# Attention's opening by halves of its heads, a fixed matmul order in two closings, and a row scale that shares a PSUM bank

## The chip, the cores and the metric

The kernel runs on one core of a Trainium2 chip. The metric is the device time of one execution in microseconds, the median of three runs. The engines are TensorE (PE in the profile, with PEld for its weight loads), VectorE (DVE), ScalarE (ACT), GpSimd (POOL) and SyncE (SP, whose queue SPq issues most DMAs). Each engine works through its own instruction list in order and waits where an operand is not ready.

## The reference, cut to what matters

One inference step of a two-layer trunk, for one prompt of 1024 tokens (16 learned meta tokens ahead) and eight samples of 4 new tokens with a paged cache.

```python
x = x + conv_module(x);  x = x + conv_ffn(rms_norm(x))         # layer 0
hn = rms_norm(h, kv_norm)
c  = rms_norm(hn @ w_dkv, lat_norm)                            # shared latent, 128 wide
kr = rope(rms_norm(hn @ w_kr, knorm_rope), pos)                # shared rotary key, 32 wide
q  = rms_norm(xn @ w_dq, q_lat_norm) @ w_uq                    # 16 heads of 64 + 32
q_nope = rms_norm(q[..., :64]);  q_rope = rope(rms_norm(q[..., 64:]), pos)
k_nope = rms_norm(c @ w_uk);  v = c @ w_uv
o  = softmax((q_nope @ k_nope + q_rope @ kr) * SM_SCALE, causal) @ v    # prompt
x  = x + o @ w_o;  x = x + conv_ffn(rms_norm(x))               # layer 1
```

The samples attend to the same latent, read from pages of the cache. Every product of fp32 matrices is made as three matmuls over high and low parts (`mm3`, `split`).

## The kernel before, in words

The stages follow one another: convolution module, ConvFFN of layer 0, `latents`, `attention` over the prompt, `samples`, w_o, ConvFFN of layer 1. A tile framework gives out the buffers: a pool with n buffers makes the next tile wait until the tile n places earlier is no longer used, and a PSUM tile likewise. A scheduler sets the order on each engine from priorities and dependences; `self.follow(x, early)` adds an order without a wait of its own, and `manual()` keeps TensorE's instructions in the order of the code.

**Closings.** `closing` makes the last two output tiles of a projection (128 channels each, tokens in three chunks): chunks 0 and 1 of both tiles first, then chunk 2 of the one and of the other. From the second step on, the row scale of the result stands between them: `part_rstd` sums squares of all rows by matmuls against `ones` (L221, L222), VectorE makes the reciprocal root (L249 to L254), spreads it (L231), TensorE transposes it (L234) and ScalarE copies it out (L239). It runs twice: at the end of layer 0's convolution module and at the end of w_o. In the list `self.wedge` the code keeps the matmuls that the next one has to follow.

**Latents.** Nine blocks of rows go through w_dkv, w_kr and w_dq in three groups of three (`project(0)` to `project(2)`, 72 matmuls each, L958), with `norms` (ScalarE, tile `cts`, L966 and L970) and `place` (VectorE, then transposes, L986) behind each. `token_rstd` makes the row scale of all nine blocks by 18 small matmuls (L285), in a PSUM tile of its own. The pool has two such tiles of three banks.

**Attention.** Keys (`group_k`) and queries (`group_q`) are made for four heads at a time, so there are four groups. A group's keys are 27 matmuls in five units, the queries 54 in nine blocks (L146); ScalarE copies each out and squares it, VectorE sums the squares (L1103, L1141, L1142). Then VectorE makes the reciprocal root, scales keys (L1112) and queries (L1150, L1155), and applies the rotation (`rope`, L1046 to L1050). In the first group this scaling is VectorE's, in later ones mostly GpSimd's. `keys(p)` transposes the keys of two heads (L1182, L1188), `query(n)` a head's queries (L1204, L1207), `scores(n)` finds each row's maximum by 13 score matmuls (L1234) and a reduction on VectorE of each (L1236 to L1241), `shift(n)` puts the maximum into the queries (L1246, L1250), and `values(n, g)` makes the scores again, their exponentials on ScalarE (L1281), and the product with v (L1264). While the values of head n run, `query`, `scores` and `keys` of the next are issued between them, and the next group's `group_k` and `group_q` are drawn from `side`, a step at a time (`RATE` 1.3), from the ninth step of the group's first head on. Ahead of the loop stands the opening: the first group's keys and queries together, then `keys(0)`, `query(0)`, `scores(0)`, `shift(0)` and `group_v(0)`.

**Samples.** SyncE fetches the cache's pages (L560, tile `pg`, two pools); the buffers lie where attention's were, so the first pages wait for the last users of those. The first sample's work is issued beside the last head's values.

## Time and profile before

| | us |
|---|---|
| median of 3 runs (2855.44 to 2859.43) | 2856.01 |
| the profiled execution, its own time | 2864.26 |
| its span, first to last instruction | 2862.5 |
| TensorE busy / VectorE busy | 2683.4 / 1915.2 |
| ScalarE busy / GpSimd busy | 1382.6 / 658.4 |

The mean granted clock of TensorE in the profiled execution is 0.963 of full speed. Full speed is 2.4 GHz, the lower level 1.2 GHz. A busy time is the sum over an engine's instructions; the times that the prediction names as "at 1424" are microseconds from the start of this span.

### The profile page before, as it was taken

Reading aid. Unit: us, or ns where it says so; the run is one execution under the profiler, and the core shown is the slowest. Engines: PE = TensorE matmul, PEld = TensorE weight load, DVE = VectorE, ACT = ScalarE, POOL = GpSimd, SP = SyncE. Lnnn points to the kernel's source line nnn. Section 1 sums busy time; section 2 is a strip of 40 time slices with the busy share of each in tenths; the row PEclk is TensorE's granted clock in tenths of the full one; section 3 lists DMA queues with packets and bytes.
Section 4 is the critical chain, followed back from the end, with each engine's and each line's share of the span. In section 5 each row is a group of like instructions: output and inputs, shape, how many; then the busy total and the mean of one; then the engine's idle time right before and its main releaser. Section 6 shows DMA issues by size and latency. Waiting matters only on the chain.

```text
span 2862.5 us, 47478 instructions
## 1 busy us (share of the span) xinstructions
PE 2683.4 (94%) x16916; PEld 2465.8 (86%) x16916; DVE 1915.2 (67%) x3516; ACT 1382.6 (48%) x4074; POOL 658.4 (23%) x919
## 2 busy tenths in 40 slices
PE   7999986999999999999789999888999999999999
PEld 5888874999999999999666776656999999999999
DVE  8899997559888875235577767655448777776131
ACT  6767778435445453023545564545325454544010
POOL 1557542005333330001101211100004332331000
PEclk9999998999999999999889999977999999999999
DMA  4111110412322236122100001437502222227122
GB/s 135 54 38 55 38 50 20 151 47 67 98 88 92 84 105 233 39 92 89 36 5 24 31 16 31 119 114 227 193 31 70 78 78 85 75 88 252 46 84 73
DMA packets 127777, 238.30 MB, mean 83 GB/s; under 512 B 39778, under 2 KB 81140, under 8 KB 127412
## 3 DMA queue, kind: packets, MB, share of 16 engines
q1 hardware_dynamic: 103828, 200.82, 22.0%
q0 software_dynamic: 9600, 32.36, 3.1%
q10 hardware_dynamic: 14112, 2.09, 0.4%
q8 instruction: 133, 2.18, 0.3%
q14 instruction: 104, 0.85, 0.1%
HBM read 183.90 MB, written 51.31 MB: 82 GB/s over the span
## 4 chain that ended last, share of the span: by engine, by line
PE 78%; DVE 9%; ACT 5%; SPq 3%; issue 3%; DMA 3%; POOL 0%; ACTq 0%; DVEq 0%
PE ps L740 29%; PE ps L170 21%; PE v L1264 4%; PE pk L601 3%; PE ps L789 3%; PE g L393 3%; PE p L146 2%; DVE a L486 2%; ACT qq L613 2%; PE ps L192 2%; PE ps L958 1%; SPq L560 1%; SPq L558 1%; PE p L1274 1%; PE p L1276 1%
## 5 line engine op out<-in xcount | busy, mean ns | idle before, releaser
L134 ACT ACTIVATE wh<-raw 128x512 fp32r<-128x512 f32 (+2 forms) x256 | 191.4, 751 | 566.0 <-PE ps L170 363.2
L135 DVE TENSOR_TENSOR wl<-raw,wh 128x512 fp32r<-128x512 f32 (+2 forms) x244 | 201.4, 829 | 106.2 <-ACT wh L134 104.0
L886 DVE TENSOR_TENSOR x<-ps,x 128x1074 f32<-128x1074 f32 (+1 forms) x48 | 61.0, 1270 | 288.7 <-PE ps L170 288.7
L710 DVE SCALAR_TENSOR_TENSOR c<-ub,c,c 128x1040 f32<-128x1040 f32 (+1 forms) x176 | 225.5, 1314 | 30.5 <-ACT c L707 29.7
L613 ACT ACTIVATE qq<-pk 128x64 f32<-128x64 f32 x936 | 198.1, 247 | 81.6 <-PE pk L601 81.0
L613 ACT ACTIVATION_READ_ACCUMULATOR qq<-pk 128x1 f32 x936 | 194.1, 232 | 0.1
L1264 PE MATMUL v<-pf,vf 128*128 128x512 f32 (+4 forms) x448 | 174.6, 474 | 12.8 <-ACT pf L1281 12.7
L705 POOL COPY sb<-ub 128x32 f32<-128x32 f32 x88 | 87.1, 992 | 404.3 <-DVE ub L751 365.7
L608 POOL TENSOR_TENSOR sq<-sq 128x256 f32<-128x256 f32 x198 | 130.2, 659 | 185.3 <-ACT sq L604 178.0
L601 PE MATMUL pk<-ukh,ch 128*128 128x512 f32 x256 | 116.7, 457 | 46.7 <-ACT qq L613 17.3
L1281 ACT ACTIVATE pf<-p 128x512 f32<-128x512 f32 (+4 forms) x224 | 99.4, 450 | 120.8 <-DVE p L1279 99.5
L170 PE MATMUL ps<-xh,wh 128*128 128x358 f32 (+1 forms) x672 | 147.9, 329 | 4.3 <-DVE x L886 3.2
L170 PE MATMUL ps<-xh,wl 128*128 128x358 f32 (+1 forms) x672 | 147.4, 327 | 0.4 <-DVE wl L135 0.4
L170 PE MATMUL ps<-al,wh 128*128 128x358 f32 (+1 forms) x672 | 147.3, 328 | 0.0
L170 PE MATMUL ps<-xl,wh 128*128 128x358 f32 (+1 forms) x672 | 147.0, 327 | 0.0
L170 PE MATMUL ps<-ah,wl 128*128 128x358 f32 (+1 forms) x672 | 146.6, 326 | 0.0
L170 PE MATMUL ps<-ah,wh 128*128 128x358 f32 (+1 forms) x672 | 146.3, 326 | 0.0
L486 DVE SCALAR_TENSOR_TENSOR a<-u,c,a 128x512 f32<-128x512 f32 x200 | 137.9, 745 | 0.0
L707 ACT ACTIVATE c<-ub,c 128x1074 f32<-128x1074 f32 (+1 forms) x88 | 101.3, 1185 | 67.6 <-DVE ub L751 53.1
L393 PE MATMUL g<-xh,wh 128*128 128x358 f32 x336 | 113.0, 336 | 18.2 <-DVE u L377 16.4
L170 PEld LDWEIGHTS ps<-xh,wh 128*128 128x128 f32 x672 | 116.3, 190 | 6.4 <-ACT ah L134 3.8
L134 ACT ACTIVATE wh<-s 128x512 fp32r<-128x512 f32 x120 | 75.6, 630 | 92.2 <-PE ps L740 85.4
(584 smaller groups left out, 9141.0 us busy)
## 6 DMA issues: line engine op xcount, KB each, us to landing
raw<-wup SPq DMA_DIRECT2D x88, 512.0 KB, 3.5
pg<-ctn SPq DMA_DIRECT2D x128, 192.0 KB, 2.6
raw<-wdn SPq DMA_DIRECT2D x32, 448.0 KB, 3.4
raw<-pw SPq DMA_DIRECT2D x24, 512.0 KB, 3.9
d_a<-c POOLq DMA_DIRECT2D x22, 537.0 KB, 3.6
raw<-d_a SPq DMA_DIRECT2D x22, 537.0 KB, 4.8
d_a<-c POOLq DMA_DIRECT2D x22, 531.0 KB, 3.2
raw<-d_a SPq DMA_DIRECT2D x22, 531.0 KB, 5.3
```

The source lines that it names most:

```text
L134: return (nc.scalar.activation(h, src, AF.Copy), (eng or nc.vector).tensor_tensor(out=l, in0=src, in1=h.bitcast(F32), op=ALU.subtract))
L135: (eng or nc.vector).tensor_tensor(out=l, in0=src, in1=h.bitcast(F32), op=ALU.subtract))
L170: nc.tensor.matmul(p[:, c, :ch], s[:, k * 128:(k + 1) * 128], m[k][:, off + c * ch:off + (c + 1) * ch], start=k == 0 and i == 0, stop=k == ...
L393: nc.tensor.matmul(p[:, 0], x[:, k * 128:(k + 1) * 128], m[k][:, t * ch:t * ch + ch], start=k == 0 and i == 0, stop=k == KD - 1 and i == 2)
L486: nc.vector.scalar_tensor_tensor(out=p[:, :ND] if j == n - 1 else acc, in0=x[:, j:j + ND], scalar=w[:, j:j + 1], in1=p[:, :ND] if j == 1 e ...
L601: nc.tensor.matmul(ps, s[:, j, :], m[:, 512 * c:512 * c + 512], start=i == 0, stop=i == 2)
L608: nc.gpsimd.tensor_tensor(out=v[:, :, :n], in0=v[:, :, :n], in1=v[:, :, n:2 * n], op=ALU.add)
L613: nc.scalar.activation(q, ps[:, 64 * h:64 * h + 64], AF.Square, accum_out=ss[:, p, 8 * c + h:8 * c + h + 1])
L707: x = nc.scalar.activation(c, ub, AF.Copy, scale=wd[:, t, 2:3])
L710: nc.vector.scalar_tensor_tensor(out=c[:, 2:pe], in0=ub[:, tap:tap + pe - 2], scalar=wd[:, t, tap:tap + 1], in1=c[:, 2:pe], op0=ALU.mult, ...
L740: nc.tensor.matmul(ps, w[:, s], m[:, lo:hi], start=first and k == 0 and i == 0, stop=k == KD // 2 - 1 and i == 2, skip_group_check=True)
L1264: nc.tensor.matmul(o[:, at_:], vf[:m, b, c], p[:m, :512 - at_], start=b == 0, stop=last)
```

## The change

Three parts. In `closing` the last matmul of each step is put into `self.wedge`, so that the next step's matmuls follow it and the order on TensorE is that of the code. In `latents` the row scale's small matmuls are written into the last bank of `project(0)`'s PSUM tile, from column 420 on, after that projection's last matmul, and `project(1)` gets the tile that the row scale had. In `attention` the opening is rewritten: keys of the first group, then its queries' matmuls, then scaling and rotation for the first two heads, their `keys`, `query` and `scores`, then scaling and rotation for the other two heads (the scaling of these on GpSimd); the nine blocks of the second group's queries are issued in the opening (`nxt`), and the loop's first `side` is `group_k(1)` with what is left of `nxt`. The pools are grouped anew, and PSUM's pool pair is taken apart, so that the first units can use two of its three buffers alone.

```diff
 closing:
+                self.wedge.append(x)
                 with self.tc.high_priority(PRIO):
 token_rstd:
-    def token_rstd(self, pool, blocks):
+    def token_rstd(self, pool, blocks, ps=None, at=256, early=()):
-        ps = self.pp.tile([128, 3, 512], F32, name="ps")
+        ps = self.pp.tile([128, 3, 512], F32, name="ps") if ps is None else ps
-        t = ps[:, 2, 256:256 + 2 * NB]
+        t = ps[:, 2, at:at + 2 * NB]
...
 latents:
+                self.wedge = [x]
                 return ps
...
-            r9, _ = self.token_rstd(cp, [sq[:, 18 + 128 * b:146 + 128 * b] for b in range(8)] + [sq8])
+            r9, _ = self.token_rstd(cp, [sq[:, 18 + 128 * b:146 + 128 * b] for b in range(8)] + [sq8], p[0], 420, self.wedge)
...
 attention:
+        ag, au, am, at, al, av = [self.pool(es, n, 1) for n in ("ag", "au", "am", "at", "al", "av")]
...
+        ps_q, ps_f = self.pool(es, "ps_q", 1, space=PSUM), self.pool(es, "ps_p", NPS[1] - 1, space=PSUM)
...
+            for p in () if g else range(2):
+                for m, b0, nb in ((64, 8, 1), (128, 0, 8)):
...
+                    x = (nc.gpsimd if p else nc.vector).tensor_tensor(out=v, in0=v, in1=s, op=ALU.mult)
+                    if p:
+                        self.follow(x, st["half"])
+                yield
...
+            for r in () if g else range(2):
+                for m, b0, nb in ((64, 8, 1), (128, 0, 8)):
...
+                    yield from chunk(v, s, m, b0, nb, 2, nc.gpsimd if r else nc.vector)
+                st["half"] = () if r else [st["rope"]]
+                yield "half"
...
+        gk, gq = group_k(0), group_q(0)
+        for _ in range(7):
+            next(gk)
+        for i in range(10):
+            next(gq)
+        next(gk)
+        while next(gq) != "half":
+            pass
...
-        for i, _ in enumerate(zip_longest(group_q(0), group_k(0))):
...
         shift(0)
         group_v(0)
+        for _ in chain(gk, gq):
+            pass
+        nxt = group_q(1)
+        for _ in range(10):
+            next(nxt)
...
-                    side = both(g + 1)
+                    side = both(g + 1) if g else chain(group_k(1), nxt)
```

TensorE in the latents, before, around the row scale (`ps` is the PSUM tile with its number, `wc` the weights, `xh` and `xl` the halves of x, `x8h` and `x8l` those of the ninth block):

```order
L958 MATMUL ps_17406<-wc_17387,xl7_17247 128x416 x2
L958 MATMUL ps_17406<-wc_17387,x8h_17302 64x416
L958 MATMUL ps_17406<-wc_17387,xh7_17246 128x416 x2
L285 MATMUL ps_17479<-ones_59,sq_16697 128x2 x7
L285 MATMUL ps_17479<-ones_59,sq8_17304 128x2
L958 MATMUL ps_17539<-wc0_17310,xh0_16693 128x416 x3
L958 MATMUL ps_17539<-wc0_17310,xl0_16694 128x416 x3
L958 MATMUL ps_17539<-wc0_17310,xh0_16693 128x416 x3
```

After:

```order
L960 MATMUL ps_17406<-wc_17387,xl7_17247 128x416 x2
L960 MATMUL ps_17406<-wc_17387,x8h_17302 64x416
L960 MATMUL ps_17406<-wc_17387,xh7_17246 128x416 x2
L287 MATMUL ps_17406<-ones_59,sq_16697 128x2 x8
L287 MATMUL ps_17406<-ones_59,sq8_17304 128x2
L960 MATMUL ps_17538<-wc_17321,xl1_16773 128x416
L960 MATMUL ps_17538<-wc_17321,xh1_16772 128x416 x3
L960 MATMUL ps_17538<-wc_17332,xh2_16851 128x416 x3
```

The row scale moves from tile 17479 into `project(0)`'s tile 17406, behind all of its matmuls; `project(1)` writes tile 17538, of which 14 matmuls stand ahead of this place, between the first matmuls of `project(0)`.

TensorE at the end of the opening's projections, before (`k` and `q` are the scaled keys and queries, `uv` the weights of v, `wq` of the queries):

```order
L146 MATMUL p<-wq1l,qlh_17270 64x384
L146 MATMUL p<-wq1h,qll_17272 64x384
L1182 MATMUL s<-c_58,k 128x128 x8
L1188 MATMUL p<-c_58,k 128x64
L1204 MATMUL s<-c_58,q_17959 96x128 x8
L1234 MATMUL s<-k2h_17950,qh 128x144
L1234 MATMUL s<-k2h_17950,qh 128x272
L1207 MATMUL p<-c_58,q_17959 96x64
L146 MATMUL p<-uvh,cth 128x256
L146 MATMUL p<-uvl,cth 128x256
```

After, around the first head's queries:

```order
L147 MATMUL p<-uvh,cth 128x256
L147 MATMUL p<-uvl,cth 128x256
L147 MATMUL p<-uvh,ctl 128x256
L1220 MATMUL s<-c_58,q_18032 96x128 x8
L147 MATMUL p<-uvh,cth 16x256
L147 MATMUL p<-uvl,cth 16x256
L147 MATMUL p<-uvh,ctl 16x256
L147 MATMUL p<-wq0h,qlh_17269 128x384
L147 MATMUL p<-wq0l,qlh_17269 128x384
L147 MATMUL p<-wq0h,qll_17271 128x384
L147 MATMUL p<-wq1h,qlh_17270 128x384
```

The keys' transposes (L1182, now L1198) stand further ahead, between the blocks of the query projection; v's matmuls stand ahead of the query transposes (L1204, now L1220), and the second group's query projection begins right behind them. The values of the first head stand behind all nine of these blocks and behind the second head's score matmuls.

VectorE, before, from the queries' row scale on (`scr` is scratch, `tab` the rotation's tables):

```order
L254 SCALAR_TENSOR_TENSOR rrq<-nr_t,nr_y 128x72
L1150 TENSOR_TENSOR q_17959<-q_17959,rrq 128x8x2x64
L1155 TENSOR_TENSOR scr<-q_17959,rrq 128x512
L1150 TENSOR_TENSOR q_17959<-q_17959,rrq 128x8x2x64
L1150 TENSOR_TENSOR q_17959<-q_17959,rrq 64x2x2x64
L1046 TENSOR_TENSOR scr<-scr,tabqcos_17294 128x256
L1046 TENSOR_TENSOR scr<-scr,tabqsin_17300 128x256
L1046 TENSOR_TENSOR scr<-scr,tabqsin_17296 128x256
L1046 TENSOR_TENSOR scr<-scr,tabqcos_17298 128x256
L1049 TENSOR_TENSOR q_17959<-scr 128x8x2x16
L1050 TENSOR_TENSOR q_17959<-scr 128x8x2x16
L1155 TENSOR_TENSOR scr<-q_17959,rrq 128x512
```

After:

```order
L256 SCALAR_TENSOR_TENSOR rrq<-nr_t,nr_y 128x72
L1153 TENSOR_TENSOR q_18032<-q_18032,rrq 64x2x64
L1158 TENSOR_TENSOR scr<-q_18032,rrq 64x64
L1153 TENSOR_TENSOR q_18032<-q_18032,rrq 128x8x2x64
L1050 TENSOR_TENSOR scr<-scr,tabqcos_17294 64x32
L1050 TENSOR_TENSOR scr<-scr,tabqsin_17300 64x32
L1050 TENSOR_TENSOR scr<-scr,tabqsin_17296 64x32
L1050 TENSOR_TENSOR scr<-scr,tabqcos_17298 64x32
L1053 TENSOR_TENSOR q_18032<-scr 64x2x16
L1054 TENSOR_TENSOR q_18032<-scr 64x2x16
L1158 TENSOR_TENSOR scr<-q_18032,rrq 128x512
L1050 TENSOR_TENSOR scr<-scr,tabqcos_17294 128x256
```

The scaling of 128x8x2x64 elements comes once instead of twice, and the rotation's first piece of 128 rows finishes with both halves of the blocks in it, but with two heads of four.

## Rows read from the trace of the kernel before

**Rows 1.** Busy time of each engine in the page: us, share of the span, instructions.

```profile
PE 2683.4 (94%) x16916; PEld 2465.8 (86%) x16916; DVE 1915.2 (67%) x3516; ACT 1382.6 (48%) x4074; POOL 658.4 (23%) x919
```

**Rows 2.** TensorE's timeline in the latents: start, us, engine, line, shapes, idle before.

```profile
1354.54 1.84 PE L285 MATMUL ps<-ones,sq 128*128 128x2 f32 x16
...
1360.44 1.41 PE L958 MATMUL ps<-wc,xh 128*128 128x416 f32 x3 [4.06 <-ACT cts L966]
...
1364.36 0.73 PE L958 MATMUL ps<-wc,xl 128*128 128x416 f32 x3
...
1375.81 1.20 PE L986 MATMUL ps<-c,cts 64*128 64x64 f32 x9
...
1377.57 0.66 PE L958 MATMUL ps<-wc,xh 128*128 128x416 f32 x2 [0.56 <-ACT cts L966]
```

**Rows 3.** Four stretches at attention's opening: length; PE, PEld, DVE, ACT, POOL busy; clock.

```profile
1424.00:1443.00 19.00, 3.48 (x13) 2.11 (x13) 18.61 (x53) 4.58 (x12) 1.44 (x2) 0.62 0.08 21
1443.00:1460.00 17.00, 14.77 (x64) 11.85 (x64) 12.68 (x46) 6.33 (x14) 0.00 (x0) 0.70 0.00 1
1460.00:1482.00 22.00, 21.82 (x108) 16.46 (x108) 13.21 (x42) 13.35 (x27) 0.00 (x0) 0.94 0.02 7
1482.00:1515.00 33.00, 32.26 (x170) 25.43 (x170) 23.13 (x92) 21.65 (x60) 5.40 (x7) 1.00 0.06 17
```

**Rows 4.** What TensorE waited for, 1424 to 1443: total, times, longest.

```profile
PE s L1204 <- DVE q L1050: 8.7, 1, 8.7
PE s L1182 <- DVE k L1112: 4.8, 2, 4.6
```

**Rows 5.** VectorE's timeline at the end of the opening's preparation.

```profile
1423.83 0.48 DVE L1141 TENSOR_REDUCE ssq<-scr 128x2 f32<-128x128 f32 x2
1424.22 0.28 DVE L1142 TENSOR_REDUCE ssq<-scr 128x4 f32<-128x128 f32 x1
...
1427.22 2.68 DVE L1112 TENSOR_TENSOR k<-k,rrk 128x1024 f32<-128x1024 f32 x3
...
1434.15 0.23 DVE L254 SCALAR_TENSOR_TENSOR rrq<-nr_t,nr_y 128x72 f32<-128x72 f32 x1
1434.42 1.23 DVE L1150 TENSOR_TENSOR q<-q,rrq 128x1024 f32<-128x1024 f32 x1
...
1442.82 0.41 DVE L1050 TENSOR_TENSOR q<-scr 128x256 f32<-128x256 f32 x1
```

**Rows 6.** TensorE's timeline, one block of the second group's query projection.

```profile
1489.16 0.34 PE L146 MATMUL p<-wq0h,qlh 128*128 128x384 f32 x1
...
1490.03 0.34 PE L146 MATMUL p<-wq1h,qll 128*128 128x384 f32 x1
```

**Rows 7.** VectorE's timeline, rope of the second group.

```profile
1522.95 1.13 DVE L1046 TENSOR_TENSOR scr<-scr,tabqcos 128x256 f32<-128x256 f32 x1
1524.00 2.87 DVE L1046 TENSOR_TENSOR scr<-scr,tabqsin 128x256 f32<-128x256 f32 x2
```

**Rows 8.** GpSimd's timeline over the same stretch.

```profile
1521.35 5.24 POOL L1150 TENSOR_TENSOR q<-q,rrq 128x1024 f32<-128x1024 f32 x3 [0.47 <-DVE mx L1241]
```

**Rows 9.** TensorE's timeline in the two closings.

```profile
600.66 0.43 PE L192 MATMUL ps<-xh,wl 128*128 128x358 f32 x1 [0.26 <-DVE rs L249]
...
603.71 0.66 PE L234 MATMUL ps<-c,rx 128*128 128x128 f32 x4 [1.15 <-DVE rx L231]
...
2114.86 0.66 PE L192 MATMUL ps<-xh,wl 128*128 128x354 f32 x1 [0.26 <-DVE rs L249]
...
2119.13 0.66 PE L234 MATMUL ps<-c,rx 128*128 128x128 f32 x4 [0.95 <-DVE rx L231]
```

**Rows 10.** ScalarE's timeline at the last head.

```profile
1848.48 0.63 ACT L134 ACTIVATE ch<-pg 128x512 fp32r<-128x512 f32 x1 [1.98 <-POOL o L1311]
```

**Rows 11.** TensorE's timeline at the last head.

```profile
1855.88 0.79 PE L146 MATMUL sn<-ch,qth 128*128 128x512 f32 x1 [5.50 <-ACT qth L134]
```

**Rows 12.** What SyncE's queue waited for, 1790 to 1960.

```profile
SPq L560 <- PE p L1188: 76.0, 1, 76.0
SPq L560 <- DVE o L1297: 38.0, 1, 38.0
```

More of the change, by code (lines that the diff above doesn't have):

```diff
@@ L957, in project @@
                             m = 128 if b < 8 else 64
-                            nc.tensor.matmul(ps[:m, j, :416], x, wc[k][i // 2], start=k == 0 and i == 0,
-                                             stop=k == KD - 1 and i == 2)
+                            x = nc.tensor.matmul(ps[:m, j, :416], x, wc[k][i // 2], start=k == 0 and i == 0,
+                                                 stop=k == KD - 1 and i == 2)
+                self.wedge = [x]
                 return ps
@@ L1077, in sub, with part @@
             return bass.AP(v.tensor, v.offset + lo, [list(v.ap[0]), [224, 2 * nb], [step, 2], [1, w]])
[L1079 to L1080 removed]
+        def part(name, src, w, pool=ag):
+            raw = f32([128, w], name + "r", pool)
             nc.sync.dma_start(raw, src)
[L1082 removed]
+            h, l = f32r([128, w], name + "h", pool), f32r([128, w], name + "l", pool)
             self.split(h, l, raw)
@@ L1116, in pieces @@
-        def pieces(first, end):
-            return [x for x in ((128, 0, 4), (128, 4, 4), (64, 8, 1)) if first <= x[1] < end]
-        def group_q(g, segs=((0, 9),)):
-            q = st["qn"] = f32([128, NB, 2, 224], f"q{g % 2}", ag)
-            ss, rr = f32([128, 2, 36], "ssq"), f32([128, 2, 36], "rrq")
+            for b0 in range(0, NB, 2):
+                nb = min(2, NB - b0)
+                m = 128 if b0 < 8 else 64
+                ps = (ps_p if g else ps_f).tile([128, 512], F32, name="p")[:m, :256 * nb]
+                for j in range(nb):
+                    c0 = 128 * (b0 + j)
+                    self.mm3(ps[:, 256 * j:256 * j + 256], self.cth[:, c0:c0 + m], self.ctl[:, c0:c0 + m], uk[0], uk[1])
+                nc.scalar.activation(fl(kt[:m, b0:b0 + nb]), ps, AF.Copy)
+                sc = f32([128, 1024], "scr", bp)[:m, :256 * nb]
+                nc.scalar.activation(sc, ps, AF.Square)
+                nc.vector.tensor_reduce(out=ss[:m, 4 * b0:4 * b0 + 4 * nb], in_=sc.rearrange("p (a b) -> p a b", b=64), op=ALU.add, axis=AX.X)
+                yield
@@ new lines, in group_q, with chunk @@
+            self.rsqrt(al, rr, [((ALL, i), ss[:, i], 1.0 / n) for i, n in enumerate((64, 32))], [128, 2, 36], "qa")
+            yield
+            def chunk(v, r, m, b0, nb, c, eng):
+                s = lambda i, w: r(i).broadcast_to([m, c * nb // 2, 2, w])
+                w = v(0, 160, 64)
+                x = eng.tensor_tensor(out=w, in0=w, in1=s(0, 64), op=ALU.mult)
+                self.follow(x, st.get("half", ()))
+                yield
+                w = v(64, 64, 32)
+                t = f32([128, 1024], "scr", bp)[:m, :32 * c * nb].rearrange("p (a b) -> p a b", b=32)
+                nc.vector.tensor_tensor(out=t.rearrange("p (a c) b -> p a c b", c=2), in0=w, in1=s(1, 32), op=ALU.mult)
+                yield
+                st["rope"] = self.rope(f32([128, 1024], "scr", bp), "q", m, slice(b0, b0 + nb), c, w[:, :, :, 0:16], w[:, :, :, 16:32],
+                                       t.rearrange("p (a c) b -> p a c b", c=c))
+                yield
@@ L1161, in group_v @@
+            for m, b0, nb in PIECES if g else ():
+                s = lambda i: rr[:m, i, 4 * b0:4 * b0 + 4 * nb].rearrange("p (a c b) -> p a c b", c=2, b=1)
+                yield from chunk(lambda lo, step, w: sub(q, m, b0, nb, lo, step, w), s, m, b0, nb, 4, nc.gpsimd)
         def group_v(g):
-            uv = part("uv", a["wuv"][:, 256 * g:256 * g + 256], 256)
+            uv = part("uv", a["wuv"][:, 256 * g:256 * g + 256], 256, au)
             for b0 in (0, 2, 4, 6, 8):
```

116 lines of the change are left out of this document (44 added, 72 removed).

## The prediction

> **What bounds the kernel now.** I read the page's busy times first: TensorE is busy 2683.4 of 2862.5 us [rows 1], so nearly every microsecond that the kernel can lose is a place where TensorE stands still or runs at its lower clock, and an edit is worth what it takes from such places. Then I looked for these places where the change works. There are four. In the latents TensorE waits 4.06 us for ScalarE's copies, and the twelve matmuls behind the wait start over 3.92 us, from 1360.44 to 1364.36, where the sixty behind them take 11.45 to 1375.81, 0.191 each [rows 2]. In the opening, 1424 to 1443, TensorE is busy 3.48 of 19 us and VectorE 18.61, at a granted clock of 0.62, nearer to 1.2 GHz than to 2.4 [rows 3]; it waits 4.8 us for the scaled keys and 8.7 for the rotated queries [rows 4]. In the two closings it waits four times, 2.62 us together [rows 9]. At the last head it waits 5.50 us for the samples' query tile [rows 11]. Outside these, TensorE is full: 21.82 of 22 us and 32.26 of 33 in the two stretches of the first heads' values, 1460 to 1515 [rows 3]. So what is taken out of that last stretch and done in the opening's idle time is worth its full length, and this sets the largest term.
>
> **The change part by part.** All times are on the clock of the profiled execution, 2864.26 us, which is 8.25 above the median.
>
> *Latents.* `project(1)` waits because the pool's second tile is in use by the row scale, so it needs the tile of `project(0)`, which ScalarE has to copy out first. With the row scale in the last bank of that tile, `project(1)` has its own tile from the start: the order puts 14 of its matmuls ahead of the row scale and the other 58 directly behind, with no wait for ScalarE. The 4.06 us go [rows 2]. If the clock also stays up, twelve matmuls cost 12 x 0.191 = 2.29 instead of 3.92, another 1.63. The cost is that the row scale comes 14 x 0.191 = 2.7 us later, and the copies, squares and placing of the first group behind it too; they have some 11 us of the 58 matmuls as cover before `place(0)`'s transposes stand on TensorE, where they have 19 now (1356.4 to 1375.81). The 0.56 us ahead of `project(2)` is a wait for the second group's copies and stays. Between 4.1 (clock falls all the same) and 5.7; I take **5.7**.
>
> *Opening.* What moves: nine blocks of the second group's query projection. One block's first and sixth matmul start 0.87 us apart [rows 6], 0.174 each, so 54 matmuls are 9.4 us. They stand between the first heads' values now, in the full stretch. The order also puts the second head's scores whole ahead of the first values: 4736 columns, of which few are ahead now; at the latents' pace of 0.191 us for 416 columns an estimate of 2.1 us. Its keys' 8 transposes of the first pair of heads move too, but these were already outside the full stretch. So 11.5 us of TensorE's work leaves 1460 to 1515. The question is whether the first head's values then start later than now, at the end of the third stretch.
>
> VectorE decides it. Today its chain runs from the last query sums (0.48 and 0.28 a block [rows 5]) through the key scaling at 1427.22 (2.68), the row scale's end at 1434.15, and scaling and rotation until 1443.2. After the change the keys are done under the query projection, so 1424 to 1434 shrinks to the reciprocal root alone, and the first two heads need half of the 8.8 us from 1434.42 to 1443.2. That is about 7 plus 4 us, and the keys' load and matmuls also come earlier by some microseconds: the first queries should be ready 12 us sooner. Against it VectorE gets in front of the first values: the other half of the rotation, estimated at 4 us as its half of the 8.8; the second head's maxima, 7 us by estimate (the first head's lie within the 12.68 us of the third stretch [rows 3], with the last rotation pieces and query splits); the nine blocks' sums, 9 x 0.7 = 6. That is 17 against 12 plus the 4.3 us that VectorE is idle in 1443 to 1460. So the first values start about 1 us later than now, and the term is 11.5 - 1 = **10.5**. Bounds: no gain if VectorE, ScalarE's copies or a low clock hold the values back by 11.5 us; 15 if VectorE's parts overlap better and the clock of 0.94 in 1460 to 1482 rises.
>
> GpSimd is the edit's hidden cost. It scales the second half of keys and queries while VectorE works on the first half. The rows show what that does: the rotation's pieces of 128x256 take 0.41 us at 1442.82 [rows 5], but 1.13 and 2.87 for two while GpSimd's three multiplications run 5.24 us [rows 7, 8]; so three pieces cost 2.8 us more. Here GpSimd has half of such a set for queries and half for keys, together some 5.2 us. Nothing to 2.8 us of it falls on VectorE's first half; I count it within the 1 us above and the bounds. The Trainium skill, "SBUF — State Buffer", section "Who interferes with whom", says that a VectorE instruction with two SBUF inputs and a GpSimd instruction that reads SBUF use one interface, and that the one that comes second waits for the whole of the other. By that rule the loss could be the full 5.2 us and the opening's term 5; the trace agrees in the row of 2.87 us, and shows less than the whole.
>
> *Closings.* The ten small row-scale matmul pairs now stand behind one another and the ten large matmuls that stood between them move behind. The reciprocal root starts 1.7 us earlier and 20 instead of 10 large matmuls stand between it and the transposes. The waits of 0.26 and 1.15, and 0.26 and 0.95 [rows 9], should all be covered: **2.6** for both, 0.5 if the copy-out that stands on VectorE between them moves with them.
>
> *Last head.* ScalarE waits 1.98 us for GpSimd's normalised output at 1848.48 [rows 10], with a row of page copies in front of it and behind it, and TensorE waits 5.50 for what follows on ScalarE [rows 11]. This wait is one of memory: the copy's tile lies where that output was. With the pools regrouped the first page copies don't wait for GpSimd any longer, and the order puts six more of the last head's matmuls before the first sample product. The first pages no longer wait for the fourth pair's keys (76.0 us [rows 12]) but for earlier work; the ninth to twelfth wait for GpSimd's output instead, some 14 us later than now, with the second set of 32 not due until the attention's last output (the 38.0 us wait [rows 12]). Between +2 and -5.5; I take **3.5**.
>
> Sum: 5.7 + 10.5 + 2.6 + 3.5 = 22.3. It stays to the end, as the samples' stage begins with page fetches that wait for attention's last output, and moves with it. 2864.3 - 22.3 = 2842.0 in a profiled execution; beside the median, 2856.0 - 22.3 = **2833.7**.
>
> **The rivals.** *The opening gains little.* VectorE is busy 18.61 of 19 us there and gets more to do ahead of the first values; if the GpSimd lock costs 5 us and the maxima are paced by TensorE at its lower clock, as the 0.70 in 1443 to 1460 [rows 3] allows, the values start 8 to 11 us late and the 11.5 are given back. Then 5.7 + 2.6 + 3.5 = 11.8 stay: **2844**. Against it: the clock is low there because TensorE waits, and the moved matmuls fill these waits.
>
> *Only the waits in other places go, and the last head keeps its stall*: the later pages put it back in another form. Then 18.8: **2837**, within the forecast's range.
>
> *Slower: the clock.* The moved matmuls come in bits between VectorE's steps, six at a time, so TensorE may be active for the whole of 1430 to 1460 and still not be granted full speed, and enter the values at 1.2 GHz. The 43 us of work left in 1460 to 1515 would take twice as long while that lasts. If the low level holds for more than 22 us of that work, the whole gain is gone; for 30 us, the kernel ends 8 us above before, **2864**. For it: busy 14.77 of 17 at 0.70 in 1443 to 1460 [rows 3]. Against it: 0.94 and 1.00 directly behind, where TensorE is as full as it would be.
>
> *The change doesn't do what it says.* The order shows that it does, so this has next to nothing; only the scheduler's choice among loads could undo the early keys.
>
> **How the numbers follow.** Forecast with its own spread (2826 to 2842) 0.65; the opening gains little (2840 to 2850) 0.22; slower by the clock 0.06; about no change from several bounds at once 0.07. The range for 8 in 10 takes the forecast's and most of the first rival: 2825 to 2847. A measurement tells about 0.2%, 5.7 us, from no change, so faster is below 2850.3: 0.86; same 0.08; slower 0.06.
>
> **What would show it.** In the changed trace: no wait for ScalarE's copies ahead of `project(1)`, and `project(2)` 5 to 6 us sooner; the first queries' transposes about 12 us sooner, and TensorE busy more than 12 of the 19 us that follow the query projection; the first values at about the same distance from the latents' end as now, and the third head's values 10 us sooner; no idle time ahead of the closings' transposes; no wait of 5 us at the last head. The prediction is wrong if the first values come over 8 us late (VectorE full until then, or TensorE's clock at 1.2 GHz), if VectorE's rotation pieces in the opening take over 1 us each, or if the last head's page copies wait for GpSimd again.

## The result, and the profile after

The changed kernel takes 2841.90 us (median of five runs, 2836.05 to 2845.55), before 2856.01 (five runs, 2855.06 to 2865.11): a ratio of 0.9941, with a 95% interval of 0.9922 to 0.9961. It is faster by 16.9 us (11 to 22) by this ratio, which goes by the means of the runs (the medians are 14.1 apart), where the prediction said 22.3; the time lies in its range. The profiled execution took 2836.05 us, span 2834.3, beside 2864.26 of before; about half of these 28 us lie in stretches whose code the change doesn't touch. So the stages are compared one by one below, and not by the two ends.

The page's busy times, as [rows 1]:

```profile
PE 2675.1 (94%) x16916; PEld 2456.8 (87%) x16916; DVE 1911.5 (67%) x3521; ACT 1380.9 (49%) x4074; POOL 665.5 (23%) x923
```

TensorE's timeline in the latents of the changed kernel (start, us, engine, line, shapes, idle before), where [rows 2] had the wait of 4.06:

```profile
1344.20 2.06 PE L287 MATMUL ps<-ones,sq 128*128 128x2 f32 x18
1346.13 0.43 PE L960 MATMUL ps<-wc,xl 128*128 128x416 f32 x1
1346.40 1.30 PE L960 MATMUL ps<-wc,xh 128*128 128x416 f32 x6
...
1359.06 0.65 PE L960 MATMUL ps<-wc,xh 128*128 128x416 f32 x2 [0.56 <-ACT cts L969]
```

`project(1)` runs behind the row scale without a wait, and `project(2)` starts behind 0.56 us as before.

Stretches of the changed kernel's opening, with the columns of [rows 3] (length; PE, PEld, DVE, ACT, POOL busy; granted clock, DMA share, GB/s). The second is the stretch behind the query projection, the third to sixth have the bounds of [rows 3]:

```profile
1395.00:1403.00 8.00, 6.04 (x36) 4.91 (x35) 7.14 (x23) 7.84 (x25) 5.23 (x5) 1.00 0.00 1
1403.00:1424.00 21.00, 7.96 (x41) 7.34 (x42) 19.79 (x56) 5.52 (x17) 6.94 (x6) 0.59 0.08 20
1424.00:1443.00 19.00, 17.33 (x67) 13.63 (x66) 15.71 (x59) 6.14 (x18) 0.00 (x0) 0.73 0.02 7
1443.00:1460.00 17.00, 13.62 (x66) 10.49 (x65) 11.94 (x47) 10.51 (x27) 0.16 (x1) 0.80 0.09 25
1460.00:1482.00 22.00, 20.87 (x97) 14.31 (x96) 12.48 (x39) 14.71 (x33) 5.00 (x5) 0.95 0.01 4
1482.00:1515.00 33.00, 32.23 (x151) 23.00 (x149) 23.92 (x95) 14.62 (x33) 8.47 (x11) 0.98 0.08 20
```

TensorE's timeline in it: the first transpose of a query, and the first two matmuls of the first head's values.

```profile
1415.51 0.31 PE L1223 MATMUL p<-c,q 64*96 64x64 f32 x1 [12.35 <-DVE q L1054]
...
1448.10 0.48 PE L1290 MATMUL p<-qh,k2h 104*128 104x512 f32 x1
...
1449.96 0.45 PE L1290 MATMUL p<-qh,k2h 104*128 104x400 f32 x1 [0.71 <-ACT scr L1140]
```

One long wait of 12.35 us stands where [rows 4] had 8.7 and 4.8. Here is what VectorE did in it, and beside it GpSimd:

```profile
1405.83 3.11 DVE L254 TENSOR_TENSOR nr_t<-nr_y 128x72 f32<-128x72 f32 x1
1408.98 0.23 DVE L255 SCALAR_TENSOR_TENSOR nr_t<-nr_t,nr_v 128x72 f32<-128x72 f32 x1
1409.24 0.23 DVE L256 SCALAR_TENSOR_TENSOR nr_y<-nr_t,nr_y 128x72 f32<-128x72 f32 x1
1409.51 0.23 DVE L254 TENSOR_TENSOR nr_t<-nr_y 128x72 f32<-128x72 f32 x1
...
1412.60 2.25 DVE L1050 TENSOR_TENSOR scr<-scr,tabqcos 64x32 f32<-64x32 f32 x1
...
1414.97 0.17 DVE L1050 TENSOR_TENSOR scr<-scr,tabqcos 64x32 f32<-64x32 f32 x1
```

```profile
1405.57 1.04 POOL L1378 CAST k2l<-ktl 64x1040 fp32r<-64x1040 f32 x1
1406.59 2.26 POOL L1113 TENSOR_TENSOR k<-k,rrk 64x128 f32<-64x128 f32 x2
1411.23 3.57 POOL L1153 TENSOR_TENSOR q<-q,rrq 64x128 f32<-64x128 f32 x2 [2.38 <-DVE rrq L256]
```

The same instruction takes 3.11 us at 1405.83 and 0.23 at 1409.51, and one of 64x32 takes 2.25 and then 0.17. Both end within 0.1 us of the end of GpSimd's work beside them (1408.85 and 1414.80). That is 2.88 + 2.08 = 5.0 us on the chain that ends with the first query.

The closings and the last head on TensorE, as [rows 9] and [rows 11], and ScalarE's first page copy, as [rows 10]:

```profile
592.08 0.57 PE L193 MATMUL ps<-xh,wl 128*128 128x358 f32 x1 [0.26 <-DVE rs L251]
...
597.00 0.60 PE L236 MATMUL ps<-c,rx 128*128 128x128 f32 x4
...
2089.22 0.43 PE L193 MATMUL ps<-xh,wl 128*128 128x354 f32 x1 [0.26 <-DVE rs L251]
...
2094.10 0.60 PE L236 MATMUL ps<-c,rx 128*128 128x128 f32 x4
```

```profile
1836.94 0.50 PE L147 MATMUL sn<-ch,qth 128*128 128x512 f32 x1 [0.24 <-ACT pf L1297]
...
1869.83 1.12 PE L1585 MATMUL pp<-c,s 128*128 128x128 f32 x4 [5.73 <-ACT s L1574]
```

```profile
1831.31 0.61 ACT L135 ACTIVATE ch<-pg 128x512 fp32r<-128x512 f32 x1
```

The transposes of `rx` have no idle time ahead of them (1.15 and 0.95 before); the waits of 0.26 stay. The granted clock moves, too. The first row is of before, behind its first closing, where the changed kernel has 1.00 (604 to 608); the second is of the changed kernel, ahead of its transposes, where before has 1.00 (600 to 604):

```profile
612.00:616.00 4.00, 4.00 (x24) 4.00 (x24) 4.00 (x8) 1.95 (x3) 0.10 (x1) 0.61 0.00 0
592.00:595.60 3.60, 3.52 (x12) 3.53 (x13) 1.58 (x10) 0.00 (x0) 0.00 (x0) 0.53 0.00 0
```

The 5.50 ahead of the first sample product is 0.24, and a wait of 5.73 for ScalarE is new at 1869.83.

**Stage by stage.** The starts of the same TensorE matmuls in two traces were matched and subtracted. The table gives for each kernel (all are told below) how much shorter (-) or longer each stage is than in before, in us of one profiled execution. "First query" and "first values" are the starts of the first query transpose and of the first head's first product, counted from the end of the latents; before they stand at 1439.77 and 1458.61. This first transpose is of 64 rows in after, att, nonxt, dve2 and late, and of 128 in the others. "Gap" is the time from the one to the other. "Opening" is the end of the latents to before's 1650, by which the moved work is balanced again. "Closings" are before's 590 to 620 and 2100 to 2140, "last head" is 1797 to 2020, all to within a few us.

| kernel | closings | latents | first query | first values | gap | opening | last head |
|---|---|---|---|---|---|---|---|
| before | 0 | 0 | 0 | 0 | 18.8 | 0 | 0 |
| after | -2.5, -1.1 | -5.7 | -5.7 | +8.0 | 32.6 | -1.3 | -3.5 |
| lat | +1.7, -0.3 | -5.7 | -2.9 | -3.4 | 18.3 | -2.1 | -1.0 |
| clo | -2.6, -1.1 | +0.2 | -2.6 | -2.9 | 18.6 | +0.6 | +1.3 |
| att | +1.6, +2.8 | +0.8 | -6.5 | +6.6 | 32.0 | -5.2 | -3.4 |
| nonxt | -2.5, -2.6 | -5.7 | -6.7 | -6.1 | 19.4 | -3.4 | -4.2 |
| dve2 | -4.0, -1.1 | -5.7 | -10.6 | +3.8 | 33.3 | -8.3 | -5.6 |
| late | -2.5, -2.6 | -5.7 | -10.1 | +4.3 | 33.2 | -4.9 | -3.8 |
| big | -2.6, -2.6 | -5.7 | -4.7 | +6.9 | 30.5 | -5.1 | -4.1 |
| late_big | -2.5, -2.6 | -5.7 | -8.9 | +2.9 | 30.6 | -11.7 | -4.0 |
| dve2_big | -4.0, -1.1 | -5.7 | -8.4 | +6.6 | 33.8 | -4.4 | -5.5 |
| late_big_nonxt | -2.5, -1.1 | -5.7 | -8.8 | -8.5 | 19.1 | -6.9 | -3.1 |
| early | -4.1, -2.6 | -5.7 | -9.3 | -11.1 | 17.0 | -10.3 | -3.7 |
| early_slow | -4.1, -1.0 | -5.7 | -8.8 | -9.5 | 18.1 | -13.2 | -3.3 |

How far one execution can be trusted is seen where the code is the same: the opening is that of before in before, lat and clo, and gives 0, -2.1 and +0.6; after and att share theirs, and give -1.3 and -5.2. So a difference of some 4 us in "opening" says nothing by itself. Nor do smaller ones in the other columns: the closings come out at up to +2.8 in lat and att, which have before's, and the last head at -1.0 and +1.3 in lat and clo. "First query" and "gap" separate the kernels better.

### The profile page after: what moved, and what is told of

Read it like the earlier page. It is cut to its first block, busy times and chain, and to the rows that moved or that the text cites. A ratio compares the mean times of both kernels' runs of the same rounds, so it can differ in the third digit from the quotient of the medians.

```text
span 2834.3 us, 47489 instructions
## 1 busy us (share of the span) xinstructions
PE 2675.1 (94%) x16916; PEld 2456.8 (87%) x16916; DVE 1911.5 (67%) x3521; ACT 1380.9 (49%) x4074; POOL 665.5 (23%) x923
## 4 chain that ended last, share of the span: by engine, by line
PE 80%; DVE 7%; ACT 6%; DMA 2%; issue 2%; SPq 2%; POOL 0%; ACTq 0%; DVEq 0%
PE ps L742 29%; PE ps L171 22%; PE v L1280 5%; PE pk L603 4%; PE ps L791 3%; PE g L395 3%; PE p L147 2%; DVE a L488 2%; PE ps L193 2%; ACT qq L615 2%; PE ps L960 1%; PE p L1290 1%; PE s L1250 1%; PE p L1292 1%; PE p L1293 1%
## 5 line engine op out<-in xcount | busy, mean ns | idle before, releaser
L1280 PE MATMUL v<-pf,vf 128*128 128x512 f32 (+4 forms) x448 | 180.2, 486 | 11.8 <-ACT pf L1297 11.5
L603 PE MATMUL pk<-ukh,ch 128*128 128x512 f32 x256 | 115.2, 451 | 47.2 <-ACT qq L615 17.1
L395 PE MATMUL g<-xh,wh 128*128 128x358 f32 x336 | 111.1, 331 | 18.0 <-DVE u L379 16.2
```

What stands on the lines that cost most here:

```text
L395: nc.tensor.matmul(p[:, 0], x[:, k * 128:(k + 1) * 128], m[k][:, t * ch:t * ch + ch], start=k == 0 and i == 0, stop=k == KD - 1 and i == 2)
L603: nc.tensor.matmul(ps, s[:, j, :], m[:, 512 * c:512 * c + 512], start=i == 0, stop=i == 2)
L1280: nc.tensor.matmul(o[:, at_:], vf[:m, b, c], p[:m, :512 - at_], start=b == 0, stop=last)
```

## The experiments

**The parts alone.** *lat* is before with the hunks of `token_rstd` and `latents`, *clo* before with the line in `closing`, *att* before with the hunks of `attention`:

```diff
 lat:
-            r9, _ = self.token_rstd(cp, [... for b in range(8)] + [sq8])
+            r9, _ = self.token_rstd(cp, [... for b in range(8)] + [sq8], p[0], 420, self.wedge)
...
 clo:
+                self.wedge.append(x)
```

> The kernel before with the latents' part of the change alone: the row scale lies in the last bank of project(0)'s tile, and project(1) begins in a tile of its own; nothing else differs. Theory (the parts are independent and add up): TensorE doesn't wait ahead of project(1), project(2) comes 5.7 us sooner against the latents' beginning, and that distance stays to the end: 0.998 of before, some 2850. Rival (the latents' gain comes from the attention's loads and buffers, not from the tile): the 4 us wait stays, 1.000. In both the opening is as before: the first head's first values as far behind project(2) as there.

> The kernel before with the closings' part alone (small row-scale matmuls in one row, the large ones behind). Theory: the waits ahead of the closings' transposes go, 2.5 us in the first and 1.05 in the second as in the changed kernel, 3.5 together: 0.9988. Rival (the closings gained only because the attention's changed pools freed their tiles sooner): the second gains nothing, 0.9995 or more.

> The kernel before with the attention's part alone (opening by halves, second group's query projection as filler, buffers regrouped). Theory, from the changed kernel's trace (GpSimd's multiplications hold VectorE's row scales up for 5.0 us, and TensorE waits 12.35 us ahead of the first query's transpose): the opening gives some 2.5 us and the last head 3.6, 6.1 together: 0.9979. The prediction's own sum for the two terms was 14.0: 0.9951. Rival (the opening gains little only because the latents end sooner, so that keys and queries come later against them): the opening gives 8 us or more here, 0.996.

Measured: lat 0.9972 (0.9961 to 0.9984), 8.0 us; clo 0.9986 (0.9975 to 0.9996), 4.0 us; att 0.9971 (0.9956 to 0.9986), 8.3 us. The three add up to 20.3, within the 11 to 22 of the whole. The latents' stage is 5.7 us shorter in lat and in all ten kernels that have this part, and unchanged within 0.8 in the two that don't: the tile made the wait. The closings' part gives its 3.6 alone. The attention gives 8.3 in time, 5.2 + 3.4 in its trace, and not the 14.0 that the prediction's two terms make, whose ratio of 0.9951 lies just outside its interval. In this trace the opening is short of its 10.5 without the earlier latents, too; the time (4 to 13 us) doesn't by itself exclude the 8 us of the rival. No run takes the attention's part further apart, so what the regrouped pools give alone isn't shown.

**The filler.** *nonxt* is the changed kernel with the second group's query projection back between the heads; *late_big_nonxt* is late_big, below, with the same edit.

```diff
-        nxt = group_q(1)
-        for _ in range(10):
-            next(nxt)
...
-                    side = both(g + 1) if g else chain(group_k(1), nxt)
+                    side = both(g + 1)
```

> The changed kernel without the filler: the second group's query projection is back between the heads that it stood between before, all else as changed. Theory (moved work is worth its length where TensorE would stand still): the nine blocks, 54 matmuls or 9.4 us, come back into the full stretch behind the first values, and the first values come sooner by what VectorE's nine sums took, some 4 to 6 us: slower than the changed kernel by 3 to 6 us, 0.995 to 0.997 of before. Rival (the filler only fills the time that VectorE needs for its sums, and raises no clock): the two cancel, the same time as the changed kernel within 1.5 us. Second rival (the filler's sums are what made the first values late, all 8 us of it): faster than the changed kernel by 2 us or more.

> The kernel with both edits, without the filler: the second group's query projection is back between the heads. T3 (the filler gives back later what it costs ahead of the first values): the first values come some 12 us sooner against the latents, the stretch behind them is 12 us longer, the time is the same within 2 us: 0.9895 to 0.991. If the filler has a worth of its own once the lock is gone: slower by 3 us or more, 0.9912 and up. If its VectorE sums are the loss: faster, 0.989 or less.

Measured: nonxt 0.9929 (0.9911 to 0.9947), 2836.67 us; that isn't slower than the changed kernel, so in the change as it stands the filler has no worth that can be measured: -3 us, with an uncertainty of some 8. This excludes the 11.5 of the prediction, but not a worth of 4. late_big_nonxt has 0.9928 (0.9915 to 0.9941) where late_big has 0.9902 (0.9886 to 0.9919): there the filler seems to be worth something, some 7 us with an uncertainty of about 6. The windows of nonxt from the first key transpose to the first query, from there to the first values, and the 33 us behind:

```profile
1404.20:1422.80 18.60, 4.80 (x28) 3.88 (x28) 18.02 (x49) 7.47 (x24) 10.83 (x10) 0.69 0.08 21
1422.80:1442.30 19.50, 16.66 (x63) 12.18 (x64) 17.92 (x59) 5.55 (x12) 0.00 (x0) 0.68 0.00 1
1442.30:1475.00 32.70, 31.86 (x162) 24.25 (x162) 21.90 (x74) 22.00 (x48) 0.68 (x2) 0.95 0.03 9
```

and of the changed kernel:

```profile
1396.40:1415.50 19.10, 4.81 (x28) 3.87 (x29) 17.80 (x49) 7.94 (x25) 11.36 (x11) 0.71 0.08 21
1415.50:1448.10 32.60, 30.23 (x140) 25.76 (x140) 28.45 (x104) 14.29 (x38) 0.00 (x0) 0.75 0.02 5
1448.10:1481.00 32.90, 28.39 (x124) 19.12 (x121) 18.48 (x60) 20.65 (x47) 5.16 (x6) 0.88 0.05 13
```

The filler doesn't run in the wait ahead of the first query, where TensorE is busy 4.8 of 19 us in both. It runs in the stretch behind, which becomes 13.1 us longer, and there TensorE is now busy 30.23 of 32.60 us at a clock of 0.75. So the nine blocks, 9.4 us at the pace of [rows 6], were taken out of a full stretch and put into one that is 13 us longer with them. In it TensorE stands still for only 2.4 us. nonxt takes the blocks' sums off VectorE as well (28.45 us busy, 17.92 without), so it doesn't show what the matmuls alone cost.

**GpSimd's lock and the order of the queries.** By the lock I mean that a VectorE instruction ends only when GpSimd's work beside it does, as in the rows above. *dve2* scales the second halves on VectorE; *late* puts GpSimd's multiplications behind VectorE's rotation of the first half, by a real dependence, and the queries' second half ahead of the keys'; *big* takes the 128-row piece of the queries first, so that the first query transpose in TensorE's order is one behind the matmuls of v; *late_big* and *dve2_big* have two of these.

```diff
 dve2:
-                    x = (nc.gpsimd if p else nc.vector).tensor_tensor(out=v, in0=v, in1=s, op=ALU.mult)
+                    x = nc.vector.tensor_tensor(out=v, in0=v, in1=s, op=ALU.mult)
...
-                    yield from chunk(v, s, m, b0, nb, 2, nc.gpsimd if r else nc.vector)
+                    yield from chunk(v, s, m, b0, nb, 2, nc.vector)
 late:
-                        self.follow(x, st["half"])
+                        self.behind(x, st["rope"])
...
+                for w, f in late:
+                    self.behind(nc.gpsimd.tensor_tensor(out=w, in0=w, in1=f, op=ALU.mult), st["rope"])
...
-        for _ in chain(gk, gq):
+        for _ in chain(gq, gk):
 big:
-                for m, b0, nb in ((64, 8, 1), (128, 0, 8)):
+                for m, b0, nb in ((128, 0, 8), (64, 8, 1)):
```

> The changed kernel with the second halves of keys and queries scaled on VectorE, not on GpSimd: nothing of GpSimd runs between VectorE's row scales. Theory T1 (GpSimd's multiplications hold up two small VectorE instructions, 3.11 us for one of 128x72 and 2.25 for one of 64x32, 5.0 more than elsewhere, and these stand on the chain to the first queries): both take 0.25 us or less here, VectorE has some 2.6 us more of its own, partly behind the first half, and the first query's transpose comes 2.4 to 5 us sooner; the kernel is 2 to 4 us faster than the changed one. Rival T2 (VectorE's volume ahead of the first values, not the lock, sets their start): first queries sooner, but the first values at the same distance from the latents or later by 2.6; time the same or 2 us slower.

> The changed kernel with GpSimd's multiplications of the second halves put behind VectorE's rotation of the first half (a real dependence), so that they run under later VectorE work. T1: the two small instructions take 0.25 us or less, the first query's transpose comes 5 us sooner, and GpSimd's 5 us are met again only where VectorE then has other instructions (up to 5 us lost behind the first query, off the path if the first head's maxima wait for TensorE): 2 to 5 us faster than the changed kernel. T2: the loss only moves behind the first query and the first values start as late as in the changed kernel: same time within 1.5 us.

> The changed kernel with the piece of 128 rows ahead of the piece of 64 in both halves of the queries, so that the first query transpose in TensorE's order is one that stands behind the matmuls of the values' projection. T2 (in the changed kernel TensorE waits 12.35 us for the 64-row query with the values' projection queued behind that transpose): the projection runs in this wait, TensorE's busy time in the 21 us behind the query projection rises from 8 to 12 us or more, and the kernel is 3 to 5 us faster. T1 (VectorE's chain ends when it ends, and what TensorE has left is not what the first values wait for): TensorE's work shifts, the first values start at the same distance from the latents; same time within 1.5 us, unless the shifted work stood behind the first values.

> Both: GpSimd's multiplications behind VectorE's first rotation, and the 128-row piece first. If lock and order each cost their own time, the gains of the two add up: 5 to 9 us faster than the changed kernel, some 2835. If only one of them counts, the same as that one alone within 1.5 us. If VectorE's volume ahead of the first values is the bound, none of the four differs from the changed kernel by over 1.5 us.

> The changed kernel with the second halves scaled on VectorE and the 128-row piece first. If lock and order add up as they did with the delayed GpSimd (0.9933 and 0.9929 alone, 0.9902 together): 0.989 to 0.9905. If VectorE's own 2.6 us of multiplications weigh when TensorE no longer waits for the small query: 0.9905 to 0.992, slower than the delayed GpSimd.

Measured: dve2 0.9916 (0.9900 to 0.9933), late 0.9933 (0.9918 to 0.9949), big 0.9929 (0.9915 to 0.9944), late_big 0.9902 (0.9886 to 0.9919), dve2_big 0.9929 (0.9916 to 0.9943). VectorE's row scale in dve2, where nothing but the cast of 1.04 us is left of GpSimd's work beside it:

```profile
1404.89 0.88 DVE L254 TENSOR_TENSOR nr_t<-nr_y 128x72 f32<-128x72 f32 x1
...
1409.41 0.17 DVE L1050 TENSOR_TENSOR scr<-scr,tabqcos 64x32 f32<-64x32 f32 x1
```

The two instructions fall from 3.11 and 2.25 to 0.88 and 0.17, 4.3 us, and TensorE's wait for the first query from 12.35 to 8.04. The first takes 3.11 us in all four kernels with the lock and 0.87 or 0.88 in all seven without it. In the table the first query comes 8.4 to 10.6 us sooner than before in the seven kernels without the lock, and 4.7 to 6.7 in the four with it. So the lock's price to the first query is shown, twice by different edits. What it makes of the kernel's time is less clear: dve2 gains 7 us on the changed kernel's ratio, late 2, with some 7 us of uncertainty for such a difference. The order (big) did not do what it was made for: the matmuls of v stand behind both query transposes now, and the wait is 13.96 us where it was 12.35, so whether v could fill it isn't settled by this run; its gain of 3 us on the changed kernel's ratio is smaller than the uncertainty. Its row on TensorE:

```profile
1416.33 1.94 PE L1220 MATMUL s<-c,q 128*96 128x128 f32 x8 [13.96 <-DVE q L1054]
```

late_big, with 2827.79 us, alone is clear of the changed kernel, with intervals that don't overlap. That the two edits add up, as I had taken it, is not confirmed: dve2_big has the same order and no lock, and gains nothing on the changed kernel that can be told. Its trace shows a clock of 0.72 in the gap and 0.91 in the 32 us behind, late_big 0.80 and 1.00:

```profile
1414.80:1445.40 30.60, 28.37 (x132) 23.91 (x132) 25.99 (x102) 14.11 (x38) 4.50 (x4) 0.80 0.02 5
1445.40:1478.00 32.60, 29.05 (x149) 20.35 (x147) 22.41 (x75) 21.98 (x50) 5.17 (x6) 1.00 0.06 17
```

**The filler in the real wait.** *early* is made from late_big: six of the nine blocks stand ahead of the first query's transposes, and the sums of squares of all nine are formed later, between the heads, from the copied queries. *early_slow* hands the second group's work out later, one block of sums at a time instead of three, and puts GpSimd's scaling of it behind the due row of maxima.

```diff
 early:
+                if g == 1:
+                    yield
+                    continue
                 sc = f32([128, 1024], "scr", bp)[:, :384]
...
+        nxt = group_q(1)
+        for _ in range(1 + AHEAD):
+            next(nxt)
         query(0)
...
 early_slow:
-                due += RATE
+                due += RATE if n > 1 else SLOW
...
+                    if g == 1:
+                        self.behind(x, st["shift"])
```

> From the kernel with both edits (GpSimd's multiplications behind VectorE's first rotation, the 128-row piece first), whose time was 0.9902 of before: six of the nine blocks of the second group's query projection now stand ahead of the first query's transposes, in the 9.8 us that TensorE waits there, and the sums of squares of all nine are formed later from the copied queries, between the heads, so that VectorE's chain stays as it is. Theory T3 (the changed kernel's filler is worth nothing because it runs between the first query and the first values, where TensorE is busy 30.2 of 32.6 us at a granted clock of 0.75; without it that stretch lasts 19.5): the stretch shrinks from 30.6 to some 22 us, the wait of 9.8 falls to under 4, and the kernel is 5 to 9 us faster than the one it is made from, 0.987 to 0.9885 of before. Rival T4 (VectorE's volume of maxima and sums sets the stretch, or the clock falls behind the filler as far as it rose before): same within 2 us, 0.9895 to 0.991. Second rival (the six blocks delay the first query's transposes by more than the wait): slower than 0.991.

> From the kernel with six blocks ahead of the first query (0.9926 of before, where 0.987 to 0.9885 was expected): its stretch from first query to first values fell from 30.6 to 17.1 us at a granted clock of 1.00, as expected, but between 1478 and 1492 GpSimd's scaling of the second group's keys and queries held VectorE's instructions up (1.64, 1.08, 1.92 and 2.87 us for ones that take 0.2 to 0.7 elsewhere) ahead of the third head's row of maxima, TensorE waited 5.3 us for that row, and its clock was 0.51 for the 9 us behind it. Here the second group's work is handed out later, and GpSimd's scaling waits (a real dependence) for the row of the head that is then due. Theory (lock and volume ahead of that row took the gain): the wait of 5.3 us goes, the 9 us run at full clock, and the kernel is 6 to 10 us faster than that one, 0.989 to 0.9905 of before. Rival (VectorE's volume over the first four heads is full, so that the loss comes back at a later row or at the second group's first query): 0.9915 or more, with a wait of 3 us or more between the heads.

Measured: early 0.9926 (0.9912 to 0.9940), early_slow 0.9912 (0.9896 to 0.9928). Beside late_big_nonxt, which has no filler, that is 1 us less, with an uncertainty of 5, and 5 us less, with one of 6. The windows of early, from the first key transpose on; the third and fourth are the 66 us behind the first values:

```profile
1401.80:1417.90 16.10, 12.88 (x64) 11.62 (x64) 15.41 (x49) 10.68 (x35) 4.97 (x6) 0.89 0.09 26
1417.90:1435.00 17.10, 14.18 (x75) 9.93 (x76) 15.31 (x57) 6.63 (x16) 4.50 (x4) 1.00 0.00 0
1435.00:1468.00 33.00, 31.59 (x157) 23.37 (x156) 22.28 (x73) 23.05 (x55) 0.68 (x2) 0.95 0.07 21
1468.00:1501.00 33.00, 26.37 (x105) 17.79 (x105) 31.15 (x107) 14.12 (x36) 11.50 (x12) 0.79 0.01 1
```

The first two do what was expected: TensorE busy 12.88 of 16.1 us ahead of the first query, the gap at 17.1 us and full clock, the first values 11.1 us sooner than before where the changed kernel has them 8.0 later. Then the fourth window loses it: VectorE is busy 31.15 of 33 us. Its rows there, and TensorE's:

```profile
1478.30 1.64 DVE L259 TENSOR_TENSOR nr_t<-nr_y 128x72 f32<-128x72 f32 x1
...
1485.28 1.92 DVE L1055 TENSOR_TENSOR scr<-scr,tabqcos 128x256 f32<-128x256 f32 x1
1487.12 2.87 DVE L1055 TENSOR_TENSOR scr<-scr,tabqsin 128x256 f32<-128x256 f32 x2
...
1490.69 1.22 DVE L1291 TENSOR_TENSOR qh<-p,pick 8x1024 fp32r<-8x1024 f32 x1
```

```profile
1491.96 0.80 PE L1315 MATMUL p<-qh,kth 104*128 104x512 f32 x1 [5.31 <-DVE qh L1291]
```

The row of maxima at 1490.69 stands behind a locked rotation: the first three rows take 5.0 us more than the same shapes in dve2 (0.23, 0.42 and 0.75), while GpSimd scales the second group beside them. So VectorE's 31.15 us hold waits for GpSimd, and are not volume alone. In early_slow that wait is gone, and the opening's stage is 2.9 us shorter than in early and the kernel 4 us faster, with an uncertainty of 6; the expected 6 to 10 us didn't come clearly. Its ratio lies between the theory's and the rival's. Its window 1496 to 1530 has VectorE busy 30.87 of 34 us and TensorE 27.46, with waits of 3.69 and 1.45 for exponentials:

```profile
1512.35 0.95 PE L1309 MATMUL v<-pf,vf 128*128 128x272 f32 x2 [3.69 <-ACT pf L1326]
```

The wait of 3.69 speaks for the rival: what is taken away at one row comes back at a later one. On VectorE a rotation piece of 2.57 us stands ahead of it, at 1507.78, beside 2.48 us of GpSimd from 1507.59, so whether VectorE's volume or the lock took the gain isn't settled. Neither beats late_big, whose ratio stays the lowest, but early_slow is not clear of it either.

## Why the prediction was right, and where its sum was off

The time was right, 0.1 us inside the forecast's own spread (2826 to 2842), by three smaller terms that came; the largest term did not.

**Latents, 5.7.** Measured 5.74, to the wait of 4.06 and the clock's 1.6, in every kernel with this part. Right by its steps.

**Closings, 2.6.** Measured 2.5 and 1.1, 3.6 together, and 4.0 alone (1 to 7). The size was right; of the waits only those ahead of the transposes went, 2.10 us, and the two of 0.26 stay. The rest is within what one execution leaves open, with the granted clock at 0.53 where before had 1.00 and at 1.00 where it had 0.61.

**Last head, 3.5.** Measured 3.5, as a sum of other parts than named, so the agreement is luck in part: the wait of 5.50 is gone, but the 20 us ahead run at a granted clock of 0.83 where before had 1.00 (before, then the changed kernel):

```profile
1797.00:1817.00 20.00, 19.42 (x93) 13.59 (x92) 13.17 (x42) 11.57 (x27) 6.21 (x6) 1.00 0.21 67
1777.00:1797.00 20.00, 19.25 (x78) 12.71 (x76) 14.16 (x43) 10.04 (x24) 6.05 (x7) 0.83 0.07 28
```

They take 3.4 us longer, in att too and in seven of the nine other kernels with this part (1 us in the two left); why isn't settled. And 5.73 for ScalarE is new.

**Opening, 10.5.** This is the term that was mis-sized: 1.3 to 5.2 in two executions, against 0, -2.1 and +0.6 where the opening is unchanged. Its steps one by one, for the changed kernel. *First query*: predicted 12 us sooner, measured 5.7. The step that failed is "Nothing to 2.8 us of it falls on VectorE's first half; I count it within the 1 us above and the bounds": the lock took 5.0 us, and without it the first query comes 8.4 to 10.6 sooner. I read the price from two rope pieces that overlap GpSimd for only a part of its run [rows 7, 8]; here small instructions began just after GpSimd's and waited for all of it. The rule that I weighed and didn't take, of the Trainium skill, "SBUF — State Buffer", section "Who interferes with whom", is borne out, in that VectorE's instruction waited for the whole of GpSimd's work: the prediction set 5.2 us beside it, and the two rows have 5.0. *From first query to first values*: predicted 17 - 4.3 = 13 us longer, measured 13.8. The sum came out, its reading is in doubt: I took it for VectorE's volume, but TensorE is busy 30.23 of the 32.60 us, at a clock of 0.75, and without the filler the same gap is 19.4 us. The moved work did not go into "the opening's idle time", the premise of the largest term: there TensorE stayed at 4.81 of 19.1 us. *The moved work*: 11.5 expected behind the first values; from there to the stage's end the changed kernel is 8.0 + 1.3 = 9.3 us shorter, at a clock of 0.88 in the 33 us behind the first values. So 10.5 less 6.3 for the late query, 0.8 for the gap and 2.2 for what came back is 1.2, the measured 1.3.

With the sizes of these single traces the sum is 5.7 + 3.6 + 3.5 + 1.3 to 5.2 = 14.1 to 18.0, beside the 16.9 of the runs. In the prediction's own terms its first rival, "the opening gains little", describes the opening: the lock and TensorE at its lower clock, both named there, and 2841.90 lies between its 2844 and the forecast, nearer to it. *TensorE busy more than 12 of the 19 us behind the query projection* was wrong: it is 7.96 of 21, since in TensorE's order the 64-row query transpose (L1223) stands ahead of the matmuls of v and of the filler; that v's matmuls stand ahead of the query transposes holds for those of 128 rows alone. The clock as a reason for a slower kernel did not come. Three of the prediction's signs went against its mechanism: the first values come 8.0 us late, at its bound of 8; a rotation piece of 64x32 takes 2.25 us, where over 1 was to prove it wrong; and the third head's values start 3.2 us later than before, counted from the end of the latents, not 10 sooner.

What stays open is how much of the lock's 4 to 5 us reaches the end: dve2, late and dve2_big remove it and differ among themselves by as much as from the changed kernel, with the clock of the stretches behind.

## What to carry to other kernels

Don't count a filler at its length: here 9.4 us of it were worth -3, 7, 1 and 5 us in four pairs of kernels, each with an uncertainty of 5 to 8 (in the last two the sums are formed later, too). Look in the order at what stands ahead of it on its engine, so that it runs in the wait, and in the windows at which stretch got longer, not only at which got shorter. Work given to GpSimd beside a chain of short VectorE instructions can cost that chain GpSimd's whole run, here 5.0 us, so try it behind the chain by a dependence, or on VectorE. And take single executions as evidence for a stage only beside others with the same code in that stage.

## What was not expected of the hardware

GpSimd's timeline in the changed kernel, one instruction a row:

```profile
1406.59 0.39 POOL L1113 TENSOR_TENSOR k<-k,rrk 64x128 f32<-64x128 f32 x1
1406.95 1.90 POOL L1113 TENSOR_TENSOR k<-k,rrk 128x1024 f32<-128x1024 f32 x1
...
1411.23 1.70 POOL L1153 TENSOR_TENSOR q<-q,rrq 64x128 f32<-64x128 f32 x1 [2.38 <-DVE rrq L256]
```

The VectorE instruction at 1405.83 waited not for one GpSimd instruction but for three that followed one another without a gap: the cast from 1405.57 to 1406.61 and the two multiplications to 1408.85. It seems to go the other way too: the same shape of 64x128 took GpSimd 0.39 us beside the keys and 1.70 beside the queries, where VectorE's multiplication of 128x1024 ran from 1411.46 to 1412.67. In late, where GpSimd's pair for the queries stands elsewhere, it takes 2.27 us against 3.57 here.

And the granted clock of the gap was 0.75 behind a stretch with TensorE busy 4.81 of 19.1 us (the changed kernel), and 1.00 behind one with 12.88 of 16.1 (early); but early_slow has 0.85 behind 12.59 of 16.2. Why isn't settled.
